# One Hymba layer on one core: gate rows issued by ScalarE, held group statistics, and the down projection's sums and first forms in other buffers

## The chip, the cores and the metric

The kernel runs on one core of one Trainium2 chip. The metric is the device time of one execution in microseconds (us), as the median over runs. The engines are named TensorE (PE in the profile, PEld for its weight loads), VectorE (DVE), ScalarE (ACT), GpSimd (POOL) and SyncE (SP). Each works through its own instructions in order; semaphores tie them together. DMA transfers are issued by an engine's queue and run beside all engines.

## The reference, cut to what matters

One layer for 128 context tokens and 2048 latent tokens, width 1024, float32:

```
h   = rmsnorm(x, norm1) * (1 + scale1) + shift1
z   = h @ w_in                     # sc_b, sc_c, sc_x, q, k, v, o, gates
y_sc = sc_b * conv3(sc_c * sc_x)   # short convolution
h_m = mlstm_bidir(q, k, v, gates)  # 4 heads of 128, chunks of 128 tokens, both directions
h_m = h_m * rsqrt(mean(h_m^2) + EPS) * mh_norm * sigmoid(o)
x   = x + gate1 * (concat(y_sc, h_m) @ w_out)
h2  = rmsnorm(x, norm2) * (1 + scale2) + shift2
a, g = split(conv3(h2 @ w_up))
x   = x + gate2 * ((silu(g) * a) @ w_down)
y   = rmsnorm(x, final_norm)
```

In each chunk and direction the mLSTM computes `s = (q k^T) * exp(dlog - m_t)`, then `num = s v + w_inter * (C q)`, a normaliser `den` from the same products, and `num / max(|den|, exp(-m_t))`. The outputs are y and the final states of the context.

## The kernel before, in words

Tokens lie along the free axis in six blocks of up to 384. Every float32 product is three matmuls on pieces: an operand is split in a rounded high part and a rest (wh and wl for weights, hH and hL, tH and tL or bh and bl for the other side), and high·high, rest·high and high·rest are added in PSUM (lines 204 to 206, 349 to 351, 1021 to 1023, 1179 to 1181).

The instructions are written by generators that are interleaved with each other (`run(g, side)` takes a step of `side` after each step of `g`; `weave` does it for the scans). A scheduler of the framework then orders the instructions of each engine by its own model, unless they are marked with `pin = tc.keep_in_program_order`, which keeps them in the order in which they are written. So the order that an engine executes doesn't follow from the source alone; the rows in the section on the change show it.

The stages, with their time in the profiled execution: modulations and start (to 75 us), projections and short convolution of blocks 3 to 5 (BB, to 318), their output gates o woven with the normalised input of blocks 0 to 2 (BA, to 370), value and gate projection `vg` of BA (370 to 427), gate phase with the K heads of BA (from 427), chunk states `Sums` (to 690), mixing `Mix` (702 to 1007), output projection and sums for the up projection (to 1130), up projection in two halves by a seven-product scheme (to 2051), down projection in the same scheme (to 2555). `out_proj`, the rest of the projections and the short convolution of BA are the filling products of the two scan stages.

**Mix.** There are 34 units, one for each chunk and pair of heads. In step i of `weave` the stages of five units are written: `second` of unit i−1 (products y, L844 and L846; denominators; the normalisation: L861 and L862 form hv, L864 squares it, L865 and L866 form the inverse root on VectorE and GpSimd, L868 scales hv twice on ScalarE), `first` of unit i (q·k products S, then L833 on VectorE, which multiplies them with the exponentials), `third` of i−3 (transposition, L876 multiplies with the output gate o), `last` of i−4 (stores to yD), `pre` and `load` of i+1, and `rows` of i+2. `rows` loads R, the gate rows of the unit from DRAM, broadcast to all 128 partitions (L812, 512 KB, four buffers); `pre` adds the mask on GpSimd (L818) and takes four exponentials on ScalarE (L822). L832 multiplies q with the other half of R on VectorE.

**Mean squares.** `out_proj` works through three groups of two blocks, eight row tiles each. After the last row tile of a group `stats` calls `inv_rms` for its blocks: TensorE sums the squares over the partitions (L127), VectorE and GpSimd form the inverse root (L130, L131).

**Sums of the down projection.** `down_sums` loads eight quarters of w_down in four pieces (L580), forms four sums and differences on VectorE and stores them to wsD. It has a pool of its own, `dsp`, with eight buffers, and is interleaved with `vg(BA)`, the gate phase and the K heads.

**Start of the down projection.** `form` loads the first tokens of u (uD) into `cur` (L1080), `parts` splits them on ScalarE (L1108) and VectorE (L1109) into bh and bl; all these buffers and those of `weights_d` lie in two pools opened after the last product of the up projection is written, at memory that the up projection used before.

Of the kernel before, what the change touches and what calls it, by code (L numbers as in the profile page):

```python
# [10 lines left out]
F32 = mybir.dt.float32  # L11
# [46 lines left out]
def hymba_kernel(ctx: ExitStack, tc: tile.TileContext, I, O):  # L58
# [46 lines left out]

    def load_w(src, n=1024):
# [14 lines left out]
    def inv_rms(ss, n, r):  # L121
# [3 lines left out]
        for i in range(nch):  # L125
            w = min(P, n - i * P)
            PE.matmul(ps[:w, i:i + 1], ss[:, i * P:i * P + w], ones[:, 0:1], start=True, stop=True)  # L127
# [184 lines left out]

    ph2 = ExitStack()
    with ExitStack() as ph1:
# [113 lines left out]
        def out_proj(grps, defer):  # L428
# [11 lines left out]
            seq = [(g, m) for g in range(len(grps)) for m in range(KT)]  # L440
            ws = [load_w(I["w_out"][m]) for _, m in seq[:2]]
            nx = load_r(grps[0], 0)
            for i, (g, m) in enumerate(seq):
# [10 lines left out]
                for b, ss, xr in zip(grp, sss, xs_):  # L454
# [9 lines left out]
                    else:  # L464
                        sq = sqp.tile([P, 384], F32, name="sq")
                        S.activation(sq[:, :n], xr[:, :n], AF.Square)
                        V.tensor_add(ss[:, :n], ss[:, :n], sq[:, :n])
# [11 lines left out]
        with tc.tile_pool(name="start", bufs=1, side="right") as stp:  # L479
# [70 lines left out]

            late()
# [14 lines left out]
        phd = ExitStack()  # L566
        dsp = phd.enter_context(tc.tile_pool(name="dsp", bufs=2, side="right"))
        pin = tc.keep_in_program_order

        def down_sums():  # L570


            n = KH * P // 2
            todo = [(m, q) for m in range(4) for q in range(2)]

            def load(m, q):
                t = []
                for i, (mm, o) in enumerate(((m + 4, n * 2), (m + 4, 0), (m, 0), (m, n * 2))):
                    x = dsp.tile([P, n], F32, name=f"a{i}")
                    pin(Q.dma_start(x, I["w_down"][mm][:, o + q * n:o + (q + 1) * n]))  # L580
                    t.append(x)
                return t

            t = load(*todo[0])
            yield
            for k, (m, q) in enumerate(todo):
                nt = load(*todo[k + 1]) if k < 7 else None
                yield
                a22, a21, a11, a12 = t
                pin(V.tensor_add(a22, a21, a22))  # L590
                pin(V.tensor_sub(a21, a11, a21))
                yield
                pin(V.tensor_sub(a11, a22, a11))
                pin(V.tensor_sub(a12, a12, a11))
                yield
                for i, x in enumerate((a22, a11, a21, a12)):
                    Q.dma_start(wsD[i, m][:, q * n:(q + 1) * n], x)
                t = nt
# [194 lines left out]
        class Mix:  # L793
# [14 lines left out]
            def rows(self):  # L808
# [3 lines left out]
                Q.dma_start(self.R.rearrange("p h k d t -> p (h k d t)"),  # L812
                            nD[r0:r0 + 2].rearrange("h k d t -> (h k d t)")[None, :].to_broadcast([P, 1024]))
# [85 lines left out]
        dsums = down_sums()  # L899
        run(vg(BA, hs, load_vg(0) + load_vg(1)), dsums)  # L900
        with tc.tile_pool(name="gt", bufs=1, side="right") as gt:
            gph = gate_phase()
            kh = heads(BA, hs, 16, kD, AF.Copy, 1.0)
            while True:
# [7 lines left out]
                next(dsums, None)  # L912
            run(kh, dsums)
        run(dsums)
        phd.close()
# [19 lines left out]
        phr.close()  # L935
        slots = {6: slot(6, "right")}
# [351 lines left out]
```

## Time and profile before

| what | us |
|---|---|
| median of the runs | 2552.94 (2552.86 to 2554.05) |
| the profiled execution | 2557.2 |
| its span | 2555.4 |
| TensorE busy | 2470.1 (97%) |
| VectorE busy | 1648.0 (64%) |
| ScalarE busy | 1115.0 (44%) |
| GpSimd busy | 564.5 (22%) |
| mean granted clock of TensorE | 0.985 |

Times of the trace count from the span's start. The span leaves out 1.8 us of the execution around it. A row of waits names the waiting engine and line, the instruction whose end released it, and then the sum of the waits, their number and the longest; a row of the timeline has start, duration, engine, line, operation, output and inputs, the number of like instructions in a run, and in brackets the idle time ahead and its releaser.

### The profile page before, as it was taken

To read this page: it belongs to the slowest core of one execution; us is meant where nothing else is said; L and a number is where in the kernel's file an instruction comes from. 1 tells how busy PE (TensorE), PEld (TensorE's weight loads), DVE (VectorE), ACT (ScalarE), POOL (GpSimd) and SP (SyncE) were. 2 spreads that over 40 slices of the span, in tenths; PEclk is the share of its full clock that TensorE was granted. 3 is DMA by queue.
4 is the path that set the end of the run, shared out by engine and by line. 5 is a ranking of instruction groups with operands and counts; after the bars stand their busy time and mean duration, and the time that the engine had idled before them with its cause. 6 is when DMAs were issued, how large, how long until landed. Compare 5 with 4: busy or idle time off the path is not lost.

```text
span 2555.4 us, 42521 instructions
## 1 busy us (share of the span) xinstructions
PE 2470.1 (97%) x16127; PEld 2366.5 (93%) x16127; DVE 1648.0 (64%) x2741; ACT 1115.0 (44%) x2035; POOL 564.5 (22%) x470
## 2 busy tenths in 40 slices
PE   8999998999999889899999999899999999999998
PEld 7999998999999889899999999788888889999998
DVE  3993245322366565778677666877777786787586
ACT  4512152222355544455445444555455554444342
POOL 2542140311243433422122111212221200000000
PEclk9999999999999989999999999999999999999999
DMA  8782149656577886775225222422222286766674
GB/s 283 246 274 92 65 163 315 204 170 181 168 218 229 251 253 210 258 251 173 83 87 168 81 74 83 152 95 84 94 96 83 87 260 212 246 205 222 187 222 131
DMA packets 281423, 444.60 MB, mean 174 GB/s; under 512 B 23282, under 2 KB 206722, under 8 KB 279554
## 3 DMA queue, kind: packets, MB, share of 16 engines
q1 hardware_dynamic: 281218, 441.88, 53.4%
q8 instruction: 127, 2.08, 0.3%
q14 instruction: 78, 0.64, 0.1%
HBM read 335.31 MB, written 106.48 MB: 173 GB/s over the span
## 4 chain that ended last, share of the span: by engine, by line
PE 79%; DMA 8%; DVE 7%; ACT 2%; issue 2%; POOL 2%; SPq 1%; DVEq 0%; POOLq 0%; ACTq 0%
PE acc L204 7%; PE acc L206 7%; PE acc L205 7%; PE pa L1021 6%; PE pa L1023 6%; PE pa L1022 6%; PE d L1180 6%; PE d L1181 6%; PE d L1179 6%; PE pb L1021 3%; PE pb L1023 3%; PE pb L1022 3%; PE pc L1021 2%; PE pc L1022 2%; PE pc L1023 2%
## 5 line engine op out<-in xcount | busy, mean ns | idle before, releaser
L204 PE MATMUL acc<-hH,wh 128*128 128x384 f32 (+1 forms) x1536 | 514.4, 335 | 9.7 <-DVE row L459 5.9
L205 PE MATMUL acc<-hL,wh 128*128 128x384 f32 (+1 forms) x1536 | 506.2, 330 | 0.0
L206 PE MATMUL acc<-hH,wl 128*128 128x384 f32 (+1 forms) x1536 | 505.8, 329 | 0.4 <-POOL wl L113 0.4
L1179 PE MATMUL d<-bh,wh 128*128 128x272 f32 x1232 | 357.3, 290 | 5.6 <-ACT bh L1108 5.6
L1180 PE MATMUL d<-bl,wh 128*128 128x272 f32 x1232 | 357.6, 290 | 0.7 <-DVE bl L1109 0.7
L1181 PE MATMUL d<-bh,wl 128*128 128x272 f32 x1232 | 357.7, 290 | 0.0
L1021 PE MATMUL pa<-tH,wh 128*128 128x288 f32 (+1 forms) x1056 | 347.9, 329 | 4.1 <-DVE raw L1035 2.0
L1023 PE MATMUL pa<-tH,wl 128*128 128x288 f32 (+1 forms) x1056 | 346.7, 328 | 1.0 <-DVE wl L294 1.0
L1022 PE MATMUL pa<-tL,wh 128*128 128x288 f32 (+1 forms) x1056 | 346.8, 328 | 0.0
L294 POOL TENSOR_TENSOR wl<-st,wh 128x512 fp32r<-128x512 f32 x132 | 184.7, 1400 | 689.0 <-ACT wh L293 660.1
L113 POOL TENSOR_TENSOR wl<-wst,wh 128x512 fp32r<-128x512 f32 (+1 forms) x160 | 233.3, 1479 | 443.2 <-ACT wh L110 427.7
L204 PEld LDWEIGHTS acc<-hH,wh 128*128 128x128 f32 x1536 | 292.2, 190 | 11.7 <-DVE row L459 5.3
L206 PEld LDWEIGHTS acc<-hH,wl 128*128 128x128 f32 x1536 | 291.2, 190 | 1.2 <-POOL wl L113 0.9
L205 PEld LDWEIGHTS acc<-hL,wh 128*128 128x128 f32 x1536 | 292.0, 190 | 0.0
L966 DVE SCALAR_TENSOR_TENSOR tt<-raw,fw,tt 128x127 f32<-128x127 f32 (+4 forms) x264 | 245.0, 949 | 4.2 <-ACT tt L972 3.1
L1179 PEld LDWEIGHTS d<-bh,wh 128*128 128x128 f32 x1232 | 233.3, 189 | 6.2 <-ACT bh L1108 6.1
L1180 PEld LDWEIGHTS d<-bl,wh 128*128 128x128 f32 x1232 | 233.6, 190 | 1.2 <-DVE bl L1109 1.0
L1181 PEld LDWEIGHTS d<-bh,wl 128*128 128x128 f32 x1232 | 233.5, 190 | 0.0
L1021 PEld LDWEIGHTS pa<-tH,wh 128*128 128x128 f32 x1056 | 198.4, 188 | 20.9 <-ACT c L1028 2.2
L1023 PEld LDWEIGHTS pa<-tH,wl 128*128 128x128 f32 x1056 | 199.0, 188 | 17.0 <-DVE wl L294 1.4
L1022 PEld LDWEIGHTS pa<-tL,wh 128*128 128x128 f32 x1056 | 198.6, 188 | 15.8 <-DVE tL L279 0.2
L293 ACT ACTIVATE wh<-s 128x512 fp32r<-128x512 f32 x176 | 110.8, 630 | 177.6 <-PE pc L1022 94.2
(235 smaller groups left out, 4848.1 us busy)
## 6 DMA issues: line engine op xcount, KB each, us to landing
st<-in_w_up SPq DMA_DIRECT2D x88, 512.0 KB, 4.0
us<-uD SPq DMA_DIRECT2D x48, 544.0 KB, 4.7
wst<-in_w_in SPq DMA_DIRECT2D x48, 512.0 KB, 4.5
uD<-tt SPq DMA_DIRECT2D x44, 544.0 KB, 2.7
R<-nD SPq DMA_DIRECT2D x34, 512.0 KB, 5.4
wm<-in_w_modr SPq DMA_DIRECT2D x32, 512.0 KB, 5.1
wst<-in_w_out SPq DMA_DIRECT2D x24, 512.0 KB, 5.4
st<-wsD SPq DMA_DIRECT2D x32, 384.0 KB, 4.3
```

The costliest lines, as they stand in the source:

```text
L113: G.tensor_sub(wl[:, a:a + n // 2], st[:, a:a + n // 2], wh[:, a:a + n // 2].bitcast(F32))
L204: PE.matmul(acc[:, :n], w_h, hH[:, k, :n], start=(k == 0), stop=False)
L205: PE.matmul(acc[:, :n], w_h, hL[:, k, :n], start=False, stop=False)
L206: PE.matmul(acc[:, :n], w_l, hH[:, k, :n], start=False, stop=(k == KT - 1))
L294: (G if on_pool else V).tensor_sub(wl, a, wh.bitcast(F32))
L966: V.scalar_tensor_tensor(o, i, w, o, op0=ALU.mult, op1=ALU.add)
L1021: PE.matmul(acc, wh[:, w], rh, start=(kk == 0 and i in (0, 1, 5)), stop=False, skip_group_check=True)
L1022: PE.matmul(acc, wh[:, w], rl, start=False, stop=False, skip_group_check=True)
L1023: PE.matmul(acc, wl[:, w], rh, start=False, stop=(kk == 3), skip_group_check=True)
L1179: PE.matmul(acc, wh[:, c], uh, start=(kk == 0), stop=False)
L1180: PE.matmul(acc, wh[:, c], ul, start=False, stop=False)
L1181: PE.matmul(acc, wl[:, c], uh, start=False, stop=(kk == KH - 1))
```

## The change

- `Mix.rows` issues the load of R from ScalarE's queue, pinned, and stands behind `second` in the weave's step (before: SyncE's queue, last in the step).
- The products of `inv_rms` are pinned where `stats` calls it, and a group's statistics are asked for one block later (`held`).
- `down_sums` uses the four `xs` buffers of the `start` pool, each holding two pieces, and is interleaved with the o heads of BB and with `vg(BA)`; it ends ahead of the gate phase. The pool `dsp` goes.
- `first_forms` loads the first forms of u into two buffers of `fpool` during the last row of the up projection; two forms remain after `weights_d(0, 0)`. The pools of the down projection are split so that the first weights and splits lie at memory that comes free earlier, and `weights_d(0, 0)` and the first splits are written ahead of the last convolution steps.

The core of the diff:

```diff
+    pin = tc.keep_in_program_order
-    def inv_rms(ss, n, r):
+    def inv_rms(ss, n, r, keep=lambda ins: ins):
-            PE.matmul(ps[:w, i:i + 1], ss[:, i * P:i * P + w], ones[:, 0:1], start=True, stop=True)
+            keep(PE.matmul(ps[:w, i:i + 1], ss[:, i * P:i * P + w], ones[:, 0:1], start=True, stop=True))
...
-                inv_rms(ss, BL[b][1], rcol(b))
+                inv_rms(ss, BL[b][1], rcol(b), pin)
...
+                    if held:
+                        stats(*held.pop())
                     if m == KT - 1 and b == grp[1 - g] and g + 1 < len(grps):
                         load_y(grps[g + 1][1])
...
-                        stats(grp, sss)
+                        held.append((grp, sss))
...
+                    for mm, oo in ((m + 4, (n * 2, 0)), (m, (0, n * 2))):
+                        x = stp.tile([P, 4, 384], F32, name="xs", bufs=4).rearrange("p a b -> p (a b)")
+                        for i, o in enumerate(oo):
+                            y = x[:, i * n:(i + 1) * n]
+                            pin(Q.dma_start(y, I["w_down"][mm][:, o + q * n:o + (q + 1) * n]))
+                            t.append(y)
...
+            dsums = down_sums()
             for b in BA:
-                run(islice(go, 4))
+                run(islice(go, 4), dsums)
                 hs[b] = make_h(b, I["x"], 0)
+            run(vg(BA, hs, load_vg(0) + load_vg(1)), dsums)
+            run(dsums)
...
-                Q.dma_start(self.R.rearrange("p h k d t -> p (h k d t)"),
-                            nD[r0:r0 + 2].rearrange("h k d t -> (h k d t)")[None, :].to_broadcast([P, 1024]))
+                pin(S.dma_start(self.R.rearrange("p h k d t -> p (h k d t)"),
+                                nD[r0:r0 + 2].rearrange("h k d t -> (h k d t)")[None, :].to_broadcast([P, 1024])))
...
-                for k, stage in ((-1, "second"), (0, "first"), (-3, "third"), (-4, "last"), (1, "pre"), (1, "load"), (2, "rows")):
+                for k, stage in ((-1, "second"), (2, "rows"), (0, "first"), (-3, "third"), (-4, "last"), (1, "pre"), (1, "load")):
...
-        dsums = down_sums()
-        run(vg(BA, hs, load_vg(0) + load_vg(1)), dsums)
...
-                next(dsums, None)
-            run(kh, dsums)
-        run(dsums)
-        phd.close()
+            run(kh)
...
+    def first_forms():
+        for cs_ in (((0, 0), (0, 1)), ((0, 2), (1, 0))):
+            f, o = fpool.tile([P, SW], F32, name="F", bufs=2), 0
+            for p, c in cs_:
+                n = (CK[c][1] - CK[c][0]) * NB
+                cur[p, c] = load_u(f[:, o:o + n], 0, p, c, 0, 0)
+                o += n
...
+            if hf and j == FT - 1 and i == 0:
+                first_forms()
...
-        dw = ph3.enter_context(tc.tile_pool(name="dw", bufs=6, side="right"))
-        db = ph3.enter_context(tc.tile_pool(name="db", bufs=3, side="right"))
+        dw, bslot = [right("dw0", 2)], [[right(f"db0{c}") for c in range(3)]]
+        bslot += [[right(f"db{i}{c}") for c in range(3)] for i in (1, 2)]
+        dw += [right("dw1", 2), right("dw2", 2)]
+        db = right("db")
...
-        nb = [[parts(form(0, 0, p, c), c) for c in range(3)] for p in range(2)]
         nw = weights_d(0, 0)
+        for c in (1, 2):
+            cur[1, c] = load_u(db.tile([P, (CK[c][1] - CK[c][0]) * NB], F32, name=f"cur{c}"), 0, 1, c, 0, 0)
+        nb = [[parts(cur[0, c], c) for c in range(3)]]
         run(cv)
+        nb.append([parts(cur[1, c], c) for c in range(3)])
```

How the instructions stand on the engines, at three places. First ScalarE in the mixing stage, before the change; the numbers are those of the buffers' tiles, R_7944 and R_8028 are the rows of two units that follow each other, and so are hv_7800 and hv_7906; the unit of R_8028 is the fourth after that of hv_7906:

```order
L861 ACTIVATE hv_7800<-y_7785,den_7796 128x128
L822 ACTIVATE R_7944<-R_7944,cols_4764 128x128
L864 ACTIVATE sj_7802,hss_7801<-hv_7800 128x128
L822 ACTIVATE R_7944<-R_7944,cols_4764 128x128 x3
L868 ACTIVATE hv_7800<-hv_7800,hss_7801 128x128 x2
L861 ACTIVATE hv_7906<-y_7891,den_7902 128x128
L864 ACTIVATE sj_7908,hss_7907<-hv_7906 128x128
L861 ACTIVATE hv_7906<-y_7891,den_7902 128x128
L864 ACTIVATE sj_7908,hss_7907<-hv_7906 128x128
L822 ACTIVATE R_8028<-R_8028,cols_4764 128x128
L868 ACTIVATE hv_7906<-hv_7906,hss_7907 128x128 x2
```

and with the change, at the same place of the program, where the unit of R_7793 is the third after that of hv_7780 and the second after that of hv_7886 (L819 is now the load of R, L829 the exponentials, L868 forms hv, L871 squares it and L875 scales it):

```order
L875 ACTIVATE hv_7780<-hv_7780,hss_7781 128x128 x2
L819 DMA R_7793<-nD_68 128x1024
L868 ACTIVATE hv_7886<-y_7871,den_7882 128x128
L871 ACTIVATE sj_7888,hss_7887<-hv_7886 128x128
L868 ACTIVATE hv_7886<-y_7871,den_7882 128x128
L829 ACTIVATE R_7793<-R_7793,cols_4757 128x128 x2
L871 ACTIVATE sj_7888,hss_7887<-hv_7886 128x128
L829 ACTIVATE R_7793<-R_7793,cols_4757 128x128 x2
L875 ACTIVATE hv_7886<-hv_7886,hss_7887 128x128 x2
L819 DMA R_7899<-nD_68 128x1024
```

The load of a unit's R has come onto ScalarE, and the exponentials stand two units later than before: the load stands behind the scalings of one unit, its exponentials ahead of the scalings of the next, and the next load behind those. Second, SyncE between the o heads of BB and `vg(BA)`, before the change, where wst_3766 is the second value/gate weight and a0 to a3 are the first pieces of the sums:

```order
L365 DMA oD_65<-row_3697 128x256
L108 DMA wst_3766<-in_w_vg 128x1056
L108 DMA wst_4429<-in_w_in 128x1024
L355 DMA vD_66<-rv_3798 128x258
L580 DMA a0_3803<-in_w_down 128x704
```

and with the change, where wst_3808 and wst_3815 are the two weights of that kind and xs the pieces of the sums:

```order
L110 DMA wst_3808<-in_w_vg 128x1056
L368 DMA oD_65<-row_3751 128x256
L585 DMA wsD_75<-xs_3486 128x704
L148 DMA xt_3758<-in_x 128x4x384
L585 DMA wsD_75<-xs_3489 128x704
L585 DMA wsD_75<-xs_3486 128x704
L585 DMA wsD_75<-xs_3489 128x704
L110 DMA wst_3815<-in_w_vg 128x1056
L568 DMA xs_3720<-in_w_down 128x704 x2
```

The second weight now stands behind four stores of sums, and three pairs of loads of w_down stand ahead of it. Third, TensorE at the start of the gate phase, before the change (L660 transposes the gate columns, L669 to L696 belong to the scans of the gates, L204 to L206 are K-head products):

```order
L206 MATMUL acc<-hH,wl 128x384
L669 MATMUL S<-ident,re 1x128 x2
L685 MATMUL S<-ones,mi 128x1
L696 MATMUL S<-ident,ro 128x128
L204 MATMUL acc<-hH,wh 128x384
```

and with the change, at the transposes (now L667; L352 to L354 are the last products of `vg(BA)`):

```order
L353 MATMUL acc<-wl,hH 128x264
L354 MATMUL acc<-wh,hL 128x264
L667 MATMUL S<-ident,fc 128x128
L667 MATMUL S<-ident,ic 128x128
L206 MATMUL acc<-hH,wh 128x384
```

Before, the transposes L660 stood behind 48 K-head products; now they follow the value/gate products directly, and the three later steps (L676, L692, L703) are each separated by 48 or more K-head products.

More of the change, by code (lines that the diff above doesn't have):

```diff
@@ L549, in first_stats, with down_sums, load @@
                     yield
+            def down_sums():
+                n = KH * P // 2
+                todo = [(m, q) for m in range(4) for q in range(2)]
+                def load(m, q):
+                    t = []
+                    for mm, oo in ((m + 4, (n * 2, 0)), (m, (0, n * 2))):
[4 more added lines that the diff above has]
+                            t.append(y)
+                    return t
+                t = load(*todo[0])
+                yield
+                for k, (m, q) in enumerate(todo):
+                    nt = load(*todo[k + 1]) if k < 7 else None
+                    yield
+                    a22, a21, a11, a12 = t
+                    pin(V.tensor_add(a22, a21, a22))
+                    pin(V.tensor_sub(a21, a11, a21))
+                    yield
+                    pin(V.tensor_sub(a11, a22, a11))
+                    pin(V.tensor_sub(a12, a12, a11))
+                    yield
+                    for i, x in enumerate((a22, a11, a21, a12)):
+                        Q.dma_start(wsD[i, m][:, q * n:(q + 1) * n], x)
+                    t = nt
             late()
@@ L953, in hymba_kernel, with load_u @@
         run(last)
+    CK = ((0, 4), (4, 8), (8, KH))
+    PN = 2 * NB
+    cur = {}
+    def load_u(x, g, p, c, j, half):
+        a, e = CK[c]
+        t0 = (2 * g + p) * PN + half * NB
+        x = x[:, :(e - a) * NB]
+        Q.dma_start(x.rearrange("p (j t) -> p j t", t=NB),
+                    uD[j * KH + a:j * KH + e, :, t0:t0 + NB].rearrange("j p t -> p j t"))
+        return x
+    def first_forms():
[5 more added lines that the diff above has]
+                o += n
     with ph2:
@@ L1106, in parts @@
             n = (CK[c][1] - CK[c][0]) * NB
-            bh, bl = (db.tile([P, n], F32R, name=f"{k}{c}") for k in ("bh", "bl"))
+            pool = bslot[next(bturn) // 3 % 3][c]
+            bh, bl = (pool.tile([P, n], F32R, name=f"{k}{c}") for k in ("bh", "bl"))
             S.activation(bh, x, AF.Copy)
```

60 lines of the change are left out of this document (12 added, 48 removed).

## The prediction

> **What bounds the kernel now.** I read the page first, then the waits of each engine, then the timeline of the stages that the change touches. From the page, the span, TensorE's busy time and the chain that ended last:
>
> ```profile
> span 2555.4 us, 42521 instructions
> PE 2470.1 (97%) x16127; PEld 2366.5 (93%) x16127; DVE 1648.0 (64%) x2741; ACT 1115.0 (44%) x2035; POOL 564.5 (22%) x470
> PE 79%; DMA 8%; DVE 7%; ACT 2%; issue 2%; POOL 2%; SPq 1%; DVEq 0%; POOLq 0%; ACTq 0%
> ```
>
> TensorE is idle for 2555.4 − 2470.1 = 85.3 us in all. No matrix product is removed, so a gain can come only out of those 85 us, while a loss has no such bound. TensorE's waits at the places that the change touches (waiting line, producer; sum, times, longest):
>
> ```profile
> PE y L846 <- DVE R L833: 18.4, 5, 6.4
> PE d L1179 <- ACT bh L1108: 5.6, 1, 5.6
> PE st L127 <- DVE rc L130: 3.5, 2, 2.2
> PE S L696 <- ACT ro L630: 3.1, 1, 3.1
> PE st L127 <- DVE o L876: 2.6, 1, 2.6
> PE S L685 <- DVE mi L681: 2.0, 1, 2.0
> PE st L127 <- DVE ss L467: 1.7, 1, 1.7
> ```
>
> All seven together are 36.9 us: the most that those places could give back. Next, whether the gate rows R are what the mixing stage waits for. GpSimd's waits, then ScalarE's, then the line that loads R (34 loads, queue time of an issue, time to landing):
>
> ```profile
> POOL R L818 <- DMA R<-nD: 85.0, 20, 11.9
> ```
>
> ```profile
> ACT R L822 <- POOL R L818: 45.8, 27, 3.2
> ```
>
> ```profile
> L812 SPq DMA_DIRECT2D R<-nD x34: 319/382/1344, 676.6 to 968.8; - x34
> DMA to landing us min/median/max: 4.6/5.4/6.4
> ```
>
> GpSimd does wait for R, but GpSimd is idle most of the time, and TensorE's wait at L846 ends with the product L833 on VectorE, not with R. What matters is when R is asked for. From the timeline, the end of unit 0's last step on ScalarE, the load of R for unit 25, the last step of unit 22 (the one three units back), the last step of unit 30, and TensorE's products of unit 33:
>
> ```profile
> 710.34 0.69 ACT L868 ACTIVATE hv<-hv,hss 128x128 f32<-128x128 f32 x2
> ...
> 892.72 0.38 SPq L812 DMA_DIRECT2D R<-nD  x1
> ...
> 906.48 0.70 ACT L868 ACTIVATE hv<-hv,hss 128x128 f32<-128x128 f32 x2 [0.51 <-POOL hss L866]
> ...
> 988.28 0.69 ACT L868 ACTIVATE hv<-hv,hss 128x128 f32<-128x128 f32 x2 [1.31 <-POOL hss L866]
> ...
> 1006.95 0.39 PE L846 MATMUL y<-v,R 128*128 128x129 f32 x2
> ```
>
> R of unit 25 is asked for 907.18 − 892.72 = 14.5 us ahead of L868 of unit 22. A unit takes (988.97 − 711.03) / 30 = 9.27 us. So R is asked for more than a unit early, and its landing is covered by that lead.
>
> **R on ScalarE's queue.** In the new order (the rows on ScalarE, ahead of this text) every load of R(u) stands right behind the scalings L868 of unit u−3, and the exponentials of R(u) stand ahead of the scalings of unit u−2, behind which stands R(u+1). ScalarE works in order, so the lead is gone and a unit becomes a closed ring: load, landing, mask add on GpSimd (L818), exponentials (L822), the rest of the normalisation, scalings, next load. Its parts from two spots of the trace, where GpSimd and ScalarE ran without waiting for a load:
>
> ```profile
> 889.44 1.28 ACT L822 ACTIVATE R<-R,cols 128x128 f32<-128x128 f32 x4 [2.31 <-POOL R L818]
> 893.80 0.37 ACT L861 ACTIVATE hv<-y,den 128x128 f32<-128x128 f32 x1 [2.67 <-DVE den L856]
> 894.58 0.31 ACT L864 ACTIVATE sj<-hv 128x128 f32<-128x128 f32 x1 [0.42 <-DVE hv L862]
> 894.80 0.19 ACT L864 ACTIVATION_READ_ACCUMULATOR sj<-hv 128x1 f32 x1
> 897.15 0.69 ACT L868 ACTIVATE hv<-hv,hss 128x128 f32<-128x128 f32 x2 [1.09 <-POOL hss L866]
> 903.38 1.28 POOL L818 TENSOR_TENSOR R<-R,maskN 128x512 f32<-128x512 f32 x1 [0.43 <-PE y L844]
> ```
>
> The new order has three kinds of unit. (A) Two exponentials lie ahead of the second square L864, two behind: from the add's start (903.38) to the end of L868 (907.18) the trace has 3.80 us with one exponential ahead; one more at 1.28/4 = 0.32 makes 4.1. (B) All four come ahead of the normalisation: add 1.28, exponentials 1.28, then 897.84 − 893.80 = 4.04, in sum 6.6. (C) In between: A's 4.1 and one square (0.31 + 0.19), one L861 (0.37) and one exponential (0.32) more, 5.3. In the order I count 8 of A, 10 of B and 13 of C: (8 × 4.1 + 10 × 6.6 + 13 × 5.3) / 31 = 5.4 us beside the landing.
>
> The landing on this queue is not in the trace: no transfer of before is issued by ScalarE. The nearest rows: the line's 4.6 as the least and 6.4 as the most that it lists, 5.4 as its median; and one load followed by GpSimd's add with no wait in between other than for it:
>
> ```profile
> 742.81 0.37 SPq L812 DMA_DIRECT2D R<-nD  x1
> 746.72 1.65 POOL L818 TENSOR_TENSOR R<-R,maskN 128x512 f32<-128x512 f32 x1 [4.61 <-DMA R<-nD]
> ```
>
> That is 3.9 us, the shortest kind. I bound the landing by 3.6 (a little under it, nothing standing ahead in its own queue) and 6.4, and take 5.0, between the least and the median of the line, since R no longer stands behind other transfers of SyncE's queue but still shares the engines with them. On the two queues the Trainium skill, "DMA: Bandwidth & Descriptors", section "Issuing engines are not separate DMA queues", says that transfers from several engines run on the same 16 DMA engines and interleave, so that a second issuer saves only issue time; by that page the landing would stay near the median, the ring would be 0.4 us a unit longer than my value, and the sum 12 us higher. This speaks against the change, and no run so far shows it. The last step of a unit before TensorE is a product on VectorE:
>
> ```profile
> L833 DVE TENSOR_TENSOR R<-S,R x34: 652/679/692, 695.2 to 999.2; 128x512 f32<-128x512 f32 x34
> ```
>
> With 5.0 a unit takes 5.0 + 5.4 = 10.4 us against 9.27. R(3) is asked for at 711.0, R(33) at 711.0 + 30 × 10.4 = 1023.0; its landing, add, exponentials and the product L833 (the row above, median 679 ns) take 5.0 + 1.28 + 1.28 + 0.7 = 8.3 more, so the products of unit 33 start at 1031.3 and not at 1006.95: **+24, say +25**. Each microsecond of landing is 30 us here; the ring breaks even at (1006.95 − 8.3 − 711.0) / 30 = 9.6 us, a landing of 4.2. With 3.6 it is 9.0 a unit and 1006.95 − 989.3 = −18, about the 18.4 of the L846 wait; with 6.0, 11.4 and +54. ScalarE's 34 issues (0.38 each) lie inside the landing; SyncE has 34 fewer, but no wait of TensorE ends at SyncE's issues in this stage.
>
> **The sums of the down projection earlier.** Their 32 loads and 32 stores stood beside value/gate projections and the gate phase; now they start in the oB heads. Stretches of 20 us, with the busy time of TensorE, its weight loads, VectorE, ScalarE and GpSimd (instructions), then TensorE's clock, DMA share and GB/s:
>
> ```profile
> 340.00:360.00 20.00, 20.00 (x126) 20.00 (x125) 10.81 (x27) 11.58 (x31) 4.97 (x8) 1.00 0.38 129
> 380.00:400.00 20.00, 18.02 (x134) 17.61 (x134) 11.87 (x20) 3.94 (x11) 5.57 (x9) 0.91 0.94 320
> 420.00:440.00 20.00, 20.00 (x134) 19.23 (x132) 12.10 (x31) 5.80 (x10) 0.54 (x4) 1.00 0.93 319
> 440.00:460.00 20.00, 13.53 (x63) 12.94 (x63) 8.73 (x24) 5.83 (x13) 2.50 (x2) 0.74 0.74 238
> ```
>
> At 340 the transfers have room; at 380 to 440 they are full. SyncE's queue and TensorE's gate phase before:
>
> ```profile
> 371.34 0.39 SPq L108 DMA_DIRECT2D wst<-in_w_vg  x1
> ...
> 376.96 3.00 SPq L580 DMA_DIRECT2D a<-in_w_down  x4
> ```
>
> ```profile
> 442.00 0.55 PE L685 MATMUL S<-ones,mi 1*128 1x1 f32 x2 [1.96 <-DVE mi L681]
> 445.67 0.47 PE L696 MATMUL S<-ident,ro 128*128 128x128 f32 x1 [3.12 <-ACT ro L630]
> 447.53 0.69 PE L204 MATMUL acc<-hH,wh 128*128 128x384 f32 x1 [1.39 <-ACT wh L110]
> ```
>
> Before, the second value/gate weight is asked for at 371.34, ahead of every load of the sums. In the new order of SyncE it stands behind the stores of the third pair, which wait for VectorE's sums, and these for their loads: I estimate an issue near 380, and 6 us more of waiting there (0 to 15). The gate phase loses its stalls L685, L696 and L204 (1.96 + 3.12 + 1.39 = 6.5), since products of the K heads now lie between its steps; but its first transposes now stand right behind the last value/gate product, without the two K-head products ahead of them, and wait for buffers that the last sums leave: 5.5 (1 to 9). Together 6 − 6.5 + 5.5 = **+5** (−8 to +18).
>
> **Mean squares a block later.** Two of the L127 waits (2.57, 2.24) lie in the mixing stage and are swallowed by the ring; outside lie 1.7 and the second of the 3.5 (1.3), and a part of what follows them: **−4** (−5 to 0), now hidden behind one more product of the output projection.
>
> **First forms of the down projection.**
>
> ```profile
> 2056.30 1.11 ACT L1108 ACTIVATE bh<-cur 128x1088 fp32r<-128x1088 f32 x1 [0.92 <-DMA cur<-uD]
> 2057.46 0.59 PE L1179 MATMUL d<-bh,wh 128*128 128x272 f32 x1 [5.63 <-ACT bh L1108]
> ```
>
> The first form is loaded when the up projection's buffers come free; now it lands during the last products, in a buffer of its own, and is split there. What is late next is the second chunk's split, behind the last raw copy: I keep 0.6 of the 5.63: **−5** (−6 to 0).
>
> **Sum.** +25 + 5 − 4 − 5 = +21. The profiled execution took 2557.2 us (1.8 around its span), 4.3 above the runs' median; 2557.2 + 21 − 4.3 = **2573.9, say 2574**.
>
> **Rivals.** *R lands early and the ring hides* (faster): the landing is at or under 4.0. For it speaks the pair 742.81/746.72; against it the line's least of 4.6. At 3.6: −18 + 5 − 4 − 5 = −22, 2531. The rule that goes with it: the Trainium skill, same page, "Queues, rings and completion order", has each DMA engine take turns between queues, so a lone R would not stand behind SyncE's; by that page 2531 is where it goes. *The parts cancel* (same): a landing of 4.2, where the ring equals before and the rest sums to −4: within 5 us of 2553. *The landing is long* (slower still): 6.0, as the line's rows up to 6.4 allow, if ScalarE's issue itself waits for R's buffer or for a transfer of SyncE: +54 − 4 = +50, 2603.
>
> **Chances.** The ring of 9.8 to 11.2 us (2556 to 2598): 0.57. Early landing 0.24, cancelling 0.11, long landing 0.08. Range 2527 to 2603: from the faster rival with a little of the gate phase's good end to the longest ring. A measurement here can tell some 0.2%, 5 us, from no change. Faster 0.25, same 0.11, slower 0.64.
>
> **What would show it.** Right: L822 on ScalarE waits for L818 in nearly all units and in sum well over 45.8; every R load is issued within 0.5 us of an L868; units 10 us apart; TensorE's waits for the product on VectorE (now a few lines further down than L833) several times 18.4. The 5.6 at the down projection falls under 2, and L685/L696 vanish while a wait of 4 to 9 appears at the gate transposes. Wrong: units under 9.3 us apart, with R landing in 4 us or less; or R loads issued well ahead of need.

## The result, and the profile after

The changed kernel is slower: 2593.84 us as the median of four runs (2588.72 to 2598.07) against 2552.9, a ratio of 1.0162 with a 95% interval of 1.0147 to 1.0177, or 41 us. The forecast was 2574 (+21), in a range of 2527 to 2603. In the slower state that some executions show, one run of one experiment below (the new place on SyncE's queue) took 4589 us at a mean granted clock of 0.869; it is left out of that kernel's median. Line numbers of the changed kernel are some 2 to 26 higher; in the mixing stage R is loaded in L819, the mask is added in L825, the exponentials are L829, the products with q L839 and with S L840, the squares L871, the scalings L875, and TensorE's products y are L851 and L853.

The page of the changed kernel, its span and busy times:

```profile
span 2592.2 us, 42515 instructions
PE 2484.8 (96%) x16127; PEld 2379.0 (92%) x16127; DVE 1645.4 (63%) x2741; ACT 1109.2 (43%) x2035; POOL 573.1 (22%) x470
```

TensorE does the same 16127 products. It is idle for 107.4 us where it was 85.3, and its products themselves take 14.7 us longer: the lost time is partly idle time and partly products at a lower clock (a mean granted clock of 0.979 where it was 0.985). Its waits (waiting line, producer; sum, times, longest):

```profile
PE acc L206 <- DVE row L462: 18.4, 8, 5.0
PE st L129 <- DVE rc L132: 11.4, 2, 9.1
PE y L853 <- DVE R L840: 8.4, 5, 4.4
PE acc L206 <- ACT cr L391: 7.7, 2, 4.3
PE y L853 <- ACT R L829: 5.5, 2, 3.5
PE S L667 <- DVE fc L660: 4.6, 1, 4.6
```

The wait at the products y went down, from 18.4 to 8.4 + 5.5. Most of the new waiting stands at the filling products, for accumulators that VectorE (L462) and ScalarE (L391) have not yet emptied, and one wait of 9.1 us at the statistics (L129). Read by itself, this table would put the blame on VectorE. ScalarE's and GpSimd's waits tell more, and the line that loads R, with those that waited for it:

```profile
ACT R L829 <- POOL R L825: 118.8, 31, 7.1
```

```profile
POOL R L825: 128.8, 31
DVE qs L839: 49.4, 20
```

31 of 34 units now have GpSimd wait for the landing of R and ScalarE for GpSimd, ScalarE for 118.8 us in sum; before, GpSimd waited in 20 units and ScalarE in 27, for 45.8 us. While an engine waits so, everything behind it in its order waits as well: the copies L391 on ScalarE, L462 on VectorE. One turn of the ring, from ScalarE's, GpSimd's and VectorE's timelines put together:

```profile
884.73 0.40 ACT L875 ACTIVATE hv<-hv,hss 128x128 f32<-128x128 f32 x1 [0.50 <-POOL hss L873]
884.74 0.33 ACTq L819 DMA_DIRECT2D R<-nD  x1
...
889.65 0.69 DVE L839 TENSOR_TENSOR qs<-R,q 128x512 f32<-128x512 f32 x1 [2.29 <-DMA R<-nD]
889.70 1.77 POOL L825 TENSOR_TENSOR R<-R,maskN 128x512 f32<-128x512 f32 x1 [5.00 <-DMA R<-nD]
...
891.51 0.40 ACT L829 ACTIVATE R<-R,cols 128x128 f32<-128x128 f32 x1 [4.53 <-POOL R L825]
...
893.67 0.71 POOL L873 TENSOR_TENSOR hss<-hss,mhalf 128x2 f32<-128x2 f32 x1 [2.20 <-DVE hss L872]
...
894.42 0.33 ACTq L819 DMA_DIRECT2D R<-nD  x1
894.47 0.68 ACT L875 ACTIVATE hv<-hv,hss 128x128 f32<-128x128 f32 x2
```

R is asked for at 884.74, VectorE and GpSimd both get it at 889.7, 4.96 us later; the add is done at 891.47, the normalisation of the older unit follows, and at 894.42 the next R is asked for. The turn is 9.7 us, one of the shorter kind. The load goes out 0.04 us after the end of GpSimd's root L873 (893.67 + 0.71 = 894.38), and the scalings L875 that stand ahead of it in ScalarE's order start only then, at 894.47: what releases the load is the root, for which the scalings wait, and not the end of the scalings.

By stage, from the timelines of the two kernels (us from the span's start; the scalings are L868 before and L875 now):

| point | before | changed | change so far |
|---|---|---|---|
| last product of the value/gate projection | 426.7 | 434.8 | +8.1 |
| first transposition for the chunk states | 496.2 | 508.2 | +12.0 |
| end of unit 0's scalings | 711.0 | 722.7 | +11.7 |
| end of unit 30's scalings | 989.0 | 1034.9 | +45.9 |
| first products y of unit 33 | 1006.9 | 1050.0 | +43.1 |
| last product of the output projection | 1114.4 | 1160.4 | +46.0 |
| last product of the up projection | 2051.8 | 2098.0 | +46.2 |
| first product of the down projection | 2057.5 | 2098.7 | +41.2 |
| span | 2555.4 | 2592.2 | +36.8 |

From unit 0 to unit 30 the ring took (1034.9 − 722.7) / 30 = 10.41 us a unit, where it was 9.27.

### The profile page after: what moved, and what is told of

Its sections match the earlier page's. It is cut to its first block, busy times and chain, and to the rows that moved or that the text cites. A ratio compares the mean times of both kernels' runs of the same rounds, so it can differ in the third digit from the quotient of the medians.

```text
span 2592.2 us, 42515 instructions
## 1 busy us (share of the span) xinstructions
PE 2484.8 (96%) x16127; PEld 2379.0 (92%) x16127; DVE 1645.4 (63%) x2741; ACT 1109.2 (43%) x2035; POOL 573.1 (22%) x470
## 4 chain that ended last, share of the span: by engine, by line
PE 52%; DVE 3%; DMA 2%; issue 1%; ACT 0%; POOL 0%; SPq 0%; DVEq 0%; ACTq 0%
PE pa L1047 6%; PE pa L1049 6%; PE pa L1048 6%; PE d L1202 6%; PE d L1203 6%; PE d L1201 6%; PE pb L1047 3%; PE pb L1048 3%; PE pb L1049 3%; PE pc L1047 2%; PE pc L1048 2%; PE pc L1049 2%; DMA tD<-F 0%; PE acc L206 0%; PE acc L208 0%
## 5 line engine op out<-in xcount | busy, mean ns | idle before, releaser
L206 PE MATMUL acc<-hH,wh 128*128 128x384 f32 (+1 forms) x1536 | 521.0, 339 | 32.1 <-DVE row L462 18.4
L208 PE MATMUL acc<-hH,wl 128*128 128x384 f32 (+1 forms) x1536 | 513.0, 334 | 0.3 <-POOL wl L115 0.3
L207 PE MATMUL acc<-hL,wh 128*128 128x384 f32 (+1 forms) x1536 | 512.5, 334 | 0.0
L206 PEld LDWEIGHTS acc<-hH,wh 128*128 128x128 f32 x1536 | 297.3, 194 | 36.8 <-DVE row L462 17.6
L208 PEld LDWEIGHTS acc<-hH,wl 128*128 128x128 f32 x1536 | 296.6, 193 | 1.1 <-POOL wl L115 0.9
```

Of the source, the lines that this page charges most:

```text
L206: PE.matmul(acc[:, :n], w_h, hH[:, k, :n], start=(k == 0), stop=False)
L207: PE.matmul(acc[:, :n], w_h, hL[:, k, :n], start=False, stop=False)
L208: PE.matmul(acc[:, :n], w_l, hH[:, k, :n], start=False, stop=(k == KT - 1))
```

## The experiments

The theory was the ring: loads of R behind the scalings of one unit, their first users ahead of the scalings of the next. Rivals were that the sums moved earlier, or the new place in the step, or ScalarE's transfers by themselves, cost the time.

### One part at a time

Four kernels each take one part of the diff above and leave the rest as before: the loads of R (`Mix.rows` and the step's order), the held statistics, the sums of the down projection, its first forms. Medians and ratios against runs of the kernel before:

| part alone | median, us | against before | ratio (95%) |
|---|---|---|---|
| loads of R | 2596.76 | +46.2 | 1.0177 (1.0158 to 1.0195) |
| statistics held | 2552.23 | +1.6 | 1.0005 (0.9993 to 1.0016) |
| sums earlier | 2560.07 | +9.5 | 1.0039 (1.0024 to 1.0053) |
| first forms | 2539.31 | −11.3 | 0.9952 (0.9937 to 0.9968) |

**Loads of R.** 

> The kernel before with only the loads of R moved onto ScalarE's queue. Ring theory (each R waits for the scalings three units back, and the scalings two units back wait for that R): 34 units 10.4 us apart where they were 9.27, unit 33's products 31 us later, 2584 us. Rival (the loss comes from the sums that were moved earlier and from what they delay, the ring is hidden by the filling products): within 5 us of 2553.

Measured: 2597, more than the ring's own 2584. The units are 10.59 us apart ((1029.5 − 711.9) / 30, from the ends of the scalings), and ScalarE waits as in the changed kernel:

```profile
ACT R L822 <- POOL R L818: 121.3, 31, 6.2
```

The rival that blames the sums falls: this kernel doesn't have them.

**Statistics held.** 

> The kernel before with only the group statistics held one block longer and their products pinned. As predicted: 4 us less, 2549. Rival (the stalls only move to the next product of the output projection, as the trace of the changed kernel hints with 2.9 us more between the mixing stage and the up projection): 2553 to 2556.

Measured: no difference. TensorE's timeline at the statistics, before and then with only this part:

```profile
941.08 0.83 PE L127 MATMUL st<-ones,ss 128*128 128x1 f32 x6 [2.57 <-DVE o L876]
946.89 1.28 PE L127 MATMUL st<-ones,ss 128*128 128x1 f32 x6 [2.24 <-DVE rc L130]
1042.09 0.94 PE L127 MATMUL st<-ones,ss 128*128 128x1 f32 x6 [1.67 <-DVE ss L467]
1049.70 0.83 PE L127 MATMUL st<-ones,ss 128*128 128x1 f32 x6 [1.28 <-DVE rc L130]
```

```profile
944.70 0.83 PE L127 MATMUL st<-ones,ss 128*128 128x1 f32 x6 [2.57 <-DVE rc L130]
1043.24 1.44 PE L127 MATMUL st<-ones,ss 128*128 128x1 f32 x6 [3.63 <-DVE rc L130]
```

The waits for the squares are gone, and the waits for L130 have grown in their place, from 3.5 to 6.2 us: 7.8 us of waiting in all before, 6.2 now. L130 reads the sums out of the one PSUM buffer `st`, and the products of the group's second block can't start until it has.

**Sums earlier.** 

> The kernel before with only the sums of the down projection moved ahead of the gate phase. The trace of the changed kernel has the chunk states start 12.5 us later with all parts together: 2565. As predicted: 5 us more, 2558. Rival (the delay in the projections is made up by an emptier DMA system in the gate phase and later): 2553.

Measured: 2560, between what was predicted and what the trace of the changed kernel had suggested. TensorE's stalls in the value/gate projection:

```profile
372.32 0.91 PE L140 MATMUL st<-ident,rc 128*128 128x128 f32 x6 [0.94 <-DVE xt L178]
387.37 0.56 PE L351 MATMUL acc<-wh,hH 128*128 128x264 f32 x1 [5.18 <-ACT xt L186]
393.50 0.59 PE L352 MATMUL acc<-wl,hH 128*128 128x264 f32 x1 [1.61 <-POOL rv L355]
```

The largest ends with the normalised input (L186), made from a load of x. The projection ends at 435.1 and the first transposition for the chunk states starts at 503.5, 7.3 later than before. The rest of the 9.5 isn't resolved: the profiled execution of this kernel took a span of 2554.3, under its own median.

**First forms.** 

> The kernel before with only the first forms of the down projection loaded and split early. As predicted: 5 us less, 2548. By the trace of the changed kernel the gap is 5.0 us shorter and the first 88 triples 3.1 us quicker, since TensorE's clock did not drop after the gap: 8 to 9 less, 2544. Rival (the loads of u during the last products delay the weights of the up projection): 2553.

Measured: 2539. The first product of the down projection of this kernel:

```profile
2044.77 0.39 PE L1200 MATMUL d<-bh,wh 128*128 128x272 f32 x1 [0.69 <-ACT raw L1058]
```

The wait is 0.69 where it was 5.63, and the first 88 triples take 33.4 us where they took 36.5. Windows of 10 us from the first product on, before and with this part alone (busy time of TensorE, its weight loads, VectorE, ScalarE, GpSimd, then the granted clock, DMA share and GB/s):

```profile
2057.46:2067.46 10.00, 9.27 (x54) 8.96 (x55) 10.00 (x10) 6.40 (x7) 0.00 (x0) 0.71 1.04 321
```

```profile
2044.77:2054.77 10.00, 10.00 (x79) 10.00 (x80) 9.96 (x10) 7.23 (x8) 0.00 (x0) 1.00 0.44 148
```

Behind the gap the clock was 0.71 and 54 products were done in 10 us instead of 79. The other kernels agree: in the five without the early first forms the gap is 5.2 to 5.6 us and the first 88 triples take 36.5 to 37.1 us, in the nine with them 0.69 and about 33.4. The shorter gap and the quicker triples, 4.9 and 3.0, make 8 of the 11.3 us; where the others are the traces don't show.

The four differences sum to +46.0 us; all parts together have +40.9.

### The loads of R put back on SyncE

Everything but the loads of R is kept:

```diff
-                pin(S.dma_start(self.R.rearrange("p h k d t -> p (h k d t)"),
+                Q.dma_start(self.R.rearrange("p h k d t -> p (h k d t)"),
...
-                for k, stage in ((-1, "second"), (2, "rows"), (0, "first"), (-3, "third"), (-4, "last"), (1, "pre"), (1, "load")):
+                for k, stage in ((-1, "second"), (0, "first"), (-3, "third"), (-4, "last"), (1, "pre"), (1, "load"), (2, "rows")):
```

> The changed kernel with only the loads of R put back on SyncE's queue, last in the step. Ring theory: the units go back to 9.2 to 9.3 us, 31 us less than the changed kernel, 2562. Rival (the loss is in the other parts): 2590.

Measured: 2550.61, ratio 1.0003 (0.9991 to 1.0015). The loss is gone to the last microsecond, and the other three parts cancel each other (+1.6 + 9.5 − 11.3 = −0.2). Units are 9.13 us apart, and ScalarE's wait is near that of before the change (45.8):

```profile
ACT R L829 <- POOL R L825: 47.5, 29, 3.3
```

### The new place, but SyncE's queue

```diff
-                pin(S.dma_start(self.R.rearrange("p h k d t -> p (h k d t)"),
+                pin(Q.dma_start(self.R.rearrange("p h k d t -> p (h k d t)"),
```

> The changed kernel with the loads of R at their new place in the step and pinned, but on SyncE's queue. Ring theory: SyncE does not wait for the scalings, so R is asked for early again and the units take 9.2 to 9.4 us: about 2562. Rival (the new place in the step costs, whichever queue issues): 2590.

Measured: 2553.13, ratio 1.0011 (0.9999 to 1.0024); units 9.04 us apart. The new place in the step by itself costs 6 us at most, and perhaps nothing. What costs is that the instruction stands on ScalarE, between the scalings of two units.

### Each R loaded twice

```diff
                 pin(S.dma_start(self.R.rearrange("p h k d t -> p (h k d t)"),
                                 nD[r0:r0 + 2].rearrange("h k d t -> (h k d t)")[None, :].to_broadcast([P, 1024])))
+                pin(S.dma_start(self.R.rearrange("p h k d t -> p (h k d t)"),
+                                nD[r0:r0 + 2].rearrange("h k d t -> (h k d t)")[None, :].to_broadcast([P, 1024])))
```

> The changed kernel with each load of R made twice, one behind the other into the same buffer, so that the second waits on ScalarE for the first to land. Ring theory: a landing more in the ring, in part beside the other steps since the exponentials now stand further back: 12 to 14 us a unit, 50 to 100 us more than the changed kernel. Rival (the added cost is that of the bytes or of the issue): 17 MB and 34 issues more, beside other work, at most 13 us more.

Measured: 2644.6 in two runs, 50.8 us more than the changed kernel; units (1087.3 − 731.2) / 30 = 11.87 us apart, just under the 12 to 14 expected. The price of the bytes and issues was bounded by 13 us, so time in which the order waits for landings is what counts.

### Asked for a unit earlier in the source

```diff
-            for i in range(-2, n + 4):
-                for k, stage in ((-1, "second"), (2, "rows"), (0, "first"), (-3, "third"), (-4, "last"), (1, "pre"), (1, "load")):
+            for i in range(-3, n + 4):
+                for k, stage in ((-1, "second"), (3, "rows"), (0, "first"), (-3, "third"), (-4, "last"), (1, "pre"), (1, "load")):
```

> The changed kernel with R asked for one unit earlier in the source (three units ahead and not two), still pinned on ScalarE. The order shows that the exponentials move ahead with it, so that a load and its exponentials again have at most the scalings of one unit between them. Ring theory: the ring stays, units of 9.8 to 10.4 us, 2580 to 2594. Rival (a longer lead in the source is what is lacking): 9.2 us, 2562.

Measured: 2587.08, ratio 1.0144 (1.013 to 1.0158); units 10.28 us apart. The scheduler drew the exponentials forward along with their load, and the ring closed again one unit earlier. A longer lead in the source isn't a longer lead in the order.

### The exponentials pinned

```diff
-                        S.activation(W[:, h, d], W[:, h, d], AF.Exp, bias=acol[:, h, d:d + 1])
+                        pin(S.activation(W[:, h, d], W[:, h, d], AF.Exp, bias=acol[:, h, d:d + 1]))
```

> The changed kernel with the four exponentials of a unit pinned as well, so that they stand behind the scalings of the unit two back and behind the next load of R; R stays on ScalarE's queue. Ring theory: the exponentials leave the ring; what is left of it is the landing, the mask add, the root on GpSimd and the scalings, 4.6 + 1.3 + 0.7 + 0.7 = 7.3 us, less than TensorE's work, so the units take 8.5 to 9.3 us: 2555 to 2562. Rival (a transfer issued by ScalarE costs by itself, by its issue time or by meeting SyncE's transfers): 10.4 us, 2590.

Measured: 2575.87, ratio 1.0097 (1.0082 to 1.0112), 18 us of the 41 back; units 10.03 us apart, neither theory's number. One turn of about mean length, from the timelines of ScalarE, VectorE and GpSimd:

```profile
808.81 0.33 ACTq L819 DMA_DIRECT2D R<-nD  x1
...
814.26 0.69 DVE L839 TENSOR_TENSOR qs<-R,q 128x512 f32<-128x512 f32 x1 [0.34 <-DMA R<-nD]
814.37 1.72 POOL L825 TENSOR_TENSOR R<-R,maskN 128x512 f32<-128x512 f32 x1 [8.02 <-DMA R<-nD]
815.85 0.31 ACT L871 ACTIVATE sj<-hv 128x128 f32<-128x128 f32 x1 [1.78 <-DVE hv L869]
816.54 0.35 DVE L869 SCALAR_TENSOR_TENSOR hv<-y,den,hv 128x128 f32<-128x128 f32 x1 [0.26 <-ACT hv L868]
817.66 0.16 DVE L872 TENSOR_SCALAR hss<-hss 128x2 f32<-128x2 f32 x1
817.97 0.99 POOL L873 TENSOR_TENSOR hss<-hss,mhalf 128x2 f32<-128x2 f32 x1 [1.88 <-DVE hss L872]
819.00 0.34 ACTq L819 DMA_DIRECT2D R<-nD  x1
```

ScalarE no longer waits for the mask add, but VectorE (L839) and GpSimd (L825) still take R as it lands, ahead of the older unit's normalisation, on which the next load depends. The ring had three strands, one on each engine that reads R, and pinning opened ScalarE's alone. In this turn of 10.19 us VectorE's strand is the long one: GpSimd has finished its add at 816.09 and waits 1.88 us for L872, which comes at the end of a normalisation that VectorE began behind L839. I had allowed 7.3 for GpSimd's strand, with a landing of 4.6, and left VectorE's out; in the mean over 30 turns the landing takes 5.55, the add 1.66 and the rest 2.82.

### A unit earlier, and all three readers pinned

The last two edits together, and:

```diff
-                G.tensor_add(W, W, bc(maskN[:, None], [P, 2, 2, P]))
+                pin(G.tensor_add(W, W, bc(maskN[:, None], [P, 2, 2, P])))
...
-                    V.tensor_tensor(self.qs, R[:, :, 1], bc(self.q2[:, :, None, :], [P, 2, 2, P]), op=ALU.mult)
+                    pin(V.tensor_tensor(self.qs, R[:, :, 1], bc(self.q2[:, :, None, :], [P, 2, 2, P]), op=ALU.mult))
```

A second kernel has the same on top of the first forms alone, without the held statistics and the early sums.

> The changed kernel with R asked for one unit earlier, still on ScalarE's queue, and with the three instructions that read R first (mask add on GpSimd, exponentials on ScalarE, product with q on VectorE) pinned, so that on each engine they stand behind the normalisation of the unit two back. Ring theory: no engine waits for a load of R ahead of a scaling on which the next load depends; units 9.0 to 9.3 us apart, as with R on SyncE: 2547 to 2555. Rival (what is left in the run with pinned exponentials, 10.0 us a unit, is the price of transfers issued by ScalarE): 2570 to 2576.

> The kernel before with the early first forms of the down projection, and with R on ScalarE asked for a unit earlier and its readers pinned. Ring theory: as the run with the first forms alone, 2539, or a few us under it where the late products of the mixing stage find R sooner. Rival (transfers issued by ScalarE cost by themselves): 2555 to 2565.

Measured: 2572.14 (ratio 1.0081, 1.0059 to 1.0104) and 2566.09 (1.0059, 1.0043 to 1.0074). Both miss the ring's number; the first is inside the rival's, the second 1 us above it. The trace says something else. GpSimd's group of adds, then TensorE's longest wait, of the first kernel:

```profile
L825 POOL TENSOR_TENSOR R<-R,maskN 128x512 f32<-128x512 f32 x34 | 44.3, 1304 | 24.9 <-PE S L836 24.9
```

```profile
PE y L851 <- DVE qs L839: 25.4, 14, 7.5
```

No add waits for a load of R any more: the idle time ahead of the adds has only one releaser, a product of TensorE. Units are still 9.57 us apart, since the pinned product L839 now stands behind VectorE's normalisation of an older unit, and TensorE waits for it. The worst case, VectorE's and TensorE's rows around it:

```profile
900.94 0.56 DVE L429 TENSOR_TENSOR hL<-xt,hH 128x384 fp32r<-128x384 f32 x1 [10.63 <-ACT hH L428]
...
902.91 0.68 DVE L839 TENSOR_TENSOR qs<-R,q 128x512 f32<-128x512 f32 x1
...
903.74 0.55 PE L851 MATMUL y<-sf,qs 128*128 128x129 f32 x1 [7.51 <-DVE qs L839]
```

VectorE waits 10.63 us for a split of a load from yD, with L839 behind it. So the ring is open, and my pinning made another wait of about its size. All waits at the products y are 30.4 us in the mixing stage, where the kernel with R back on SyncE has 13.1; these 17 us cover the 16 by which unit 33's products come later (1023.2 against 1007.4). This execution is the quickest of six, though, 8 us under their median, and what the slower ones add isn't in any trace. That transfers issued by ScalarE cost something by themselves isn't shown by any row; it isn't excluded either, since no kernel with hidden landings and free readers was tried.

### Sums beside the value/gate projection alone

```diff
-                run(islice(go, 4), dsums)
+                run(islice(go, 4))
```

This is the kernel with only the early sums, with that edit.

> The kernel before with the sums of the down projection in the new buffers, but interleaved with the value/gate projection alone and not with the output gates before it; all of them still end ahead of the gate phase. If the cost of the early sums is that loads of x and weights stand behind them in SyncE's queue: those loads are ahead again, the value/gate projection ends near 427 and the time is near 2551 to 2555. If it is the transfers' rate (23 MB at some 313 GB/s are 74 us from 377 on, so 451): the gate phase waits for the last sums, 15 to 25 us, 2565 to 2575.

Measured: 2567.3, ratio 1.0065 (1.0048 to 1.0082): slower than the early sums, as the second case has it. Yet the first holds for its own stage: the projection ends at 427.8. The time is lost behind it, at the gate transposes. TensorE's row, and VectorE's first instruction of the gate phase:

```profile
463.18 0.48 PE L664 MATMUL S<-ident,fc 128*128 128x128 f32 x1 [22.87 <-DMA wst<-in_w_in]
```

```profile
459.51 0.20 DVE L650 COPY ic<-gates 128x64 f32<-128x64 f32 x1 [4.32 <-DMA wsD<-xs]
```

TensorE's row names a weight's transfer as releaser, but VectorE's gate phase, from which the transposes get fc, itself starts only at 459.51, when a store of the sums has landed. The transfers are near full up to then: the DMA share is 0.99, 0.92, 0.90 and 0.98 in the stretches 377 to 400, 400 to 420, 420 to 440 and 440 to 451. The first transposition for the chunk states starts at 514.5 instead of 496.2. Sums that start early delay the loads of x, sums that start later hold up the gates: before the change they ran through both stages and held up neither.

The quickest kernel measured is the one with the first forms alone, 2539.31, 11 us under the kernel before.

## Why the prediction was right, point by point

**The ring on ScalarE** was right in its mechanism, its unit and its landing. I said 10.4 us a unit; it is 10.41 with all parts and 10.59 alone. The landing, from a load's issue to the start of GpSimd's add over units 3 to 32, is 5.05 us in the mean (3.7 to 7.9) where I took 5.0. The Trainium skill, "DMA: Bandwidth & Descriptors", section "Issuing engines are not separate DMA queues", has a second issuer save only issue time, and this trace agrees: 5.05 is near SyncE's median of 5.4. By the profile's own list (least, median, most), which covers a part of the loads, the landing is 3.6/4.5/6.6 on ScalarE's queue in the kernel with the loads of R alone and 3.7/4.5/6.5 on SyncE's where they are put back. The Trainium skill, same page, "Queues, rings and completion order", has each DMA engine take turns between queues, which would have given 3.6 to 4.0 as I read it; in the mean the loads didn't land like that.

The rest of the ring, 5.4 us, came out at 5.35, and that is in part luck. The 0.7 of the scalings isn't in the ring, since the load goes out with the root. In its place the add takes 1.61 us and not 1.28 (one of the prediction's own rows had 1.65), and what lies between the add and the next load 3.75 and not 3.4.

**One sign failed.** TensorE's waits for the product on VectorE were to grow to several times 18.4; they fell to 8.4 (13.9 with those put to L829). The ring reaches TensorE by another path, the accumulators of the filling products, and by products at a lower clock. The prediction's bound, a gain only out of 85 us of idle time, was too narrow as well, since busy time moves with the clock: with the first forms alone TensorE was busy for 2462.0 us, 8.1 less than before.

**The size was off**: +21 was forecast for all parts and 41 measured, because the term of the ring was too small, +25 against +46.2 for that part alone. The errors of the other three terms (+4.5, +5.6 and −6.3) nearly cancel. In the trace of the loads alone the products of unit 33 start at 1042.2, 35 us later than before. Two terms make the 10 us more: the ring at 10.59 and not 10.4 (30 × 0.19 = 6), and the trailing units, where I let the products of unit 33 come 8.3 us behind the last load and they came 13.4 behind (1042.2 − 1028.8): VectorE's product with S (L833) stood behind work for the filling products and ended at 1040.58, and TensorE still had filling products ahead. Of the other 11 us, 6 lie between the mixing stage and the up projection. There TensorE is idle for 13.0 us where it was 10.1, and its products take 3.3 us longer, at a mean granted clock of 0.92 and not 0.95; whether that comes from the ring or is mere variation isn't shown (the other kernels lie up to 3.4 us from the kernel before in that stretch). The rest is the difference between two profiled executions, 39 us, and the medians of many, 46: the profiled execution of before, 2557.2, was slower than its runs beside this part, 2550.61. A small slip besides: the sums for landings of 3.6 and 6.0 keep the 8.3 us of a landing of 5.0 behind the last load, which is 1.4 us too much and 1.0 too little.

**VectorE's strand was missed.** The prediction went through ScalarE and GpSimd and didn't ask which other engine reads R. It isn't seen to change the number here, but it made the run with the pinned exponentials miss.

**The early sums**: +5 predicted, +9.5 measured, inside −8 to +18. The second value/gate weight is asked for at 379.26 in the changed kernel, as estimated; the longest stall (5.25) belongs to x, whose loads stand in the same queue. The gate transposes wait 4.6, where I had 5.5.

**The held statistics**: −4 predicted, +1.6 with an interval that holds zero. The step that failed is "now hidden behind one more product of the output projection": only the wait for the squares was hidden; the second block's products wait for the PSUM buffer as before.

**The first forms**: −5 predicted, −11.3 measured. The gap went as predicted, to 0.69; what I left out is that TensorE's clock falls behind a gap, so that a wait gives back more than its length.

**The rival on the other side** (R landing at 4.0 or less) falls with the landing's mean of 5.05, *the parts cancel* as well. What came is the case called likeliest, but near the upper end of its own range of 2556 to 2598, with almost twice the forecast loss.

## What to carry to other kernels

A load put on a compute engine's queue inherits that engine's order: before moving it, list what stands ahead of the load and whether that waits, on any engine that reads the load's result, for the load before it. If it does, the landing time is paid once in every round. Where a scheduler chooses the order, asking for data earlier in the source may only move its readers as well; look at the order and not at the source.

## What the runs showed of the hardware that was not expected

- A gap costs more than its length. After 5.63 us of waiting at the start of the down projection the granted clock was 0.71 over the next 10 us (54 products instead of 79), and the first 88 triples took 3.0 us longer than where the gap was 0.69 us.
- A DMA that ScalarE issues goes out before the instructions ahead of it in ScalarE's order are done. In three kernels with the ring (all parts, the loads of R alone, R asked for a unit earlier) the loads left 0.04 us after the root for which the scalings ahead had waited, about 0.7 us before those scalings ended.
- VectorE's product L839 (0.69 us by itself) and GpSimd's add L825 (1.28 us by itself), both of 128x512 and on the same R, hardly run side by side: in the changed kernel whichever starts first takes its own time, and the other is longer by what was left of the first, less some 0.15 us. The product began first in 22 of 28 overlapping pairs, by 0.01 to 0.11 us, and the add took 1.71 to 1.81; in five the add began first, by 0.01 to 0.14 us, and took 1.26 to 1.29, the product 1.70 to 1.82. (In two other kernels three pairs, 0.02 to 0.07 us apart, went the other way round.) One pair in which the add began first:

```profile
865.76 1.26 POOL L825 TENSOR_TENSOR R<-R,maskN 128x512 f32<-128x512 f32 x1 [0.77 <-DMA R<-nD]
865.77 1.80 DVE L839 TENSOR_TENSOR qs<-R,q 128x512 f32<-128x512 f32 x1 [4.42 <-issue]
```

In the mean over 34 the add was 1335 ns before, 1600 in the changed kernel and 1304 where pinning keeps the two apart:

```profile
L825 POOL TENSOR_TENSOR R<-R,maskN 128x512 f32<-128x512 f32 x34 | 54.4, 1600 | 139.0 <-DMA R<-nD 128.8 <-PE y L853 10.2
```
